# A convolution's last loop step and three seams in a fused decoder trunk: splits, operators, squares and a norm moved

## The chip, the cores and the metric

The kernel runs on one core of a Trainium2 chip. The metric is the device time of one execution in microseconds (us). The engines are named as the profile does: PE (TensorE, matrix products; PEld its weight loads), DVE (VectorE), ACT (ScalarE), POOL (GpSimd) and SP (SyncE), whose queue issues the DMA transfers here. Each engine executes its own instructions in the order in which they were written, and waits on semaphores for others.

## The reference: two macaron layers

The reference takes x of 512 tokens x 1024 channels in float32 through two layers. Each is a half-step SwiGLU feed-forward, a token mixer, and another half-step feed-forward. The mixer of layer 0 is S5, a diagonal complex state-space layer; the one of layer 1 is a Conformer convolution. Every sublayer is normed before and after:

```python
def rmsnorm(x, g):
    y = xf * lax.rsqrt(jnp.mean(xf * xf, axis=-1, keepdims=True) + EPS)
    return (y * g).astype(x.dtype)

def conv_mixer(h, w_in, b_in, dw, dw_b, ln_g, ln_b, w_out, b_out):
    a, g = jnp.split(h @ w_in + b_in, 2, axis=-1)
    z = a * jax.nn.sigmoid(g)
    z = depthwise_conv(z, dw, width 31, causal) + dw_b
    z = jax.nn.silu(layernorm(z, ln_g, ln_b))
    return z @ w_out + b_out

for i in range(2):
    x = x + 0.5 * rmsnorm(swiglu(rmsnorm(x, pre[i, 0]), ...), post[i, 0])
    x = x + rmsnorm(mixer(rmsnorm(x, pre[i, 1])), post[i, 1])
    x = x + 0.5 * rmsnorm(swiglu(rmsnorm(x, pre[i, 2]), ...), post[i, 2])
```

(The call of the depthwise convolution is shortened.) So six sublayers follow each other: ffn0, s5, ffn2, ffn3, conv, ffn5. The numbers are those of the norms' weights.

## The kernel before

**Layout.** x stays on the chip as eight tiles of 128 channels x 512 tokens. Channels lie on partitions, so a product is `weights^T x activations` into one of 8 PSUM banks (tiles named ps, 128x512). A pool of 39 pages (pg) holds weights and activations alike, 3 raw buffers (raw) take weights as they are loaded.

**Three matmuls per product.** Weights come in units of 128x1024 floats (512 KB), loaded by SP (L90, `raw<-`w). ACT rounds a unit to a high page (L101, a cast), DVE subtracts it from the raw one to get a low page (L105). `want(n)` does this for all units up to n, in the order of the program, and asks for the loads of the three units behind each; a raw buffer is free for the next load once the subtraction has read it. Activations are split likewise: ACT makes the high part (L180), DVE the low one (L193). `mm3` (L117 to L119) then issues high x high, high x low and low x high.

**A sublayer's entry.** The first products run on x times the norm's weights, before the norm's factor is known; it is one factor y per token, multiplied in when the products leave PSUM. For it the squares of x are summed over the eight tiles on ACT (L184) and DVE (L189), `entry_norm` sums them over partitions with a matmul by ones (`stat`, L124), and three DVE steps (L132 to L134) make y.

**The seams.** `proj` is a sublayer's last product and its passage to the next. It makes 8 output tiles of 512 tokens, the last `nl` of them in two halves of 256 tokens, A and B (`nl` is 1 in the feed-forwards, 2 in S5 and the convolution). While PE does the B halves, the post-norm's stat of half A runs, and then a loop over `s` takes each half tile through scaling (`scaled`, L358), the addition to x (`added`, L362), the split into high and low part (L180, L193), and the next sublayer's first products (`entry_step`). A product's square is summed by `evac` (L273 on ACT, L278 on DVE), its values copied from PSUM by `copy` (L284, or L286 with a bias). The argument `defer` tells where the squares for the next entry norm are made: if true, behind the loop, with full width, after one more split of weights; if false, in the loop, by halves. It is true where the next sublayer is a feed-forward, which leaves it false from ffn0 to s5 and from ffn3 to conv. The work that ffn, s5 and conv hand on is in the result: pages xn, banks ps, the squares' sum acc2.

**The convolution.** Its input product gives 8 pairs of tiles (pa, pb), one per channel tile. The first two pairs are made in the seam; the loop over i = 2..7 makes the others, and runs `gate(i-1)` behind the products of step i: DVE multiplies both by y (L1148, L1150), ACT makes a sigmoid (L1149), DVE multiplies (L1153 or L1164). Tiles 0, 1 and 7 are convolved on DVE, tap by tap (`taps_dve`, L1177 to L1183, the last 5 taps of tile 7 on PE by diagonal matrices, L1194). Tiles 2 to 6 go through DRAM to be laid out anew (`z_d`, written at L1154, read at L1159), are multiplied on PE with banded matrices (`banded`, L1286, 36 matmuls of 128x128 each; the matrices are loaded by `operators`, L1277, in five transfers), leave PSUM by ACT (`unstack`, L1297) and go through DRAM again (`c_d`, L1305 and L1306, by `fetch`). `step(n)` runs n taps, `finish` and `accumulate` the sums for the layer norm. A gate's z_d and z reads, `fetch` and `operators` all issue on SP, which waits in order.

In the last step, i = 7, the order before is: products of pair 7 with the banded product of tile 4 between its two parts, `operators(5)`, `operators(6)`, `want(u0 + 19)`, `fetch`, `gate(6)`, `finish`, taps, `accumulate`, `unstack` of tile 4. `want(u0 + 19)` splits the first four units of the output weights (units 16 to 19) and asks for the loads of 19 to 22. After the loop come the banded products of tiles 5 and 6, `gate(7)`, the remaining taps and sums, and the layer norm's end: L1389 adds the last tile's parts, L1253 sums them over partitions on PE, and `lead` feeds the output projection through ACT's SiLU and copy (L1427, L1429) and DVE's low part (L1440).

Of the kernel before, what the change touches and what calls it, by code (L numbers as in the profile page):

```python
# [41 lines left out]
def trunk(ctx: ExitStack, tc: tile.TileContext, h, plan):  # L42
# [209 lines left out]

    def proj(u0, nk, rhs, post, nl, pre, xn, bias=None, lead=None, carried=None, defer=True, early=False):

# [69 lines left out]
        for m in last:  # L324
# [4 lines left out]
            copy(m, ps, A)  # L329
        psb = {}  # L330
        for i, (m, k) in enumerate((m, k) for m in last for k in range(nk)):
            if i == 5:
                sa = stat(acc[:, A])
                steps = rsqrt_steps(sa, y[:, A], carried is None)
                if pre is not None:
                    lo_engine[0] = None
                    want(un + 3)
                    lo_engine[0] = DVE
                for f in steps:
                    f()  # L340
            if k == 0:
                psb[m] = psum()[:, :n]
            product(m, k, psb[m], B)
            if k == nk - 1 and m != NK - 1:
                evac(m, psb[m], B)
                copy(m, psb[m], B)
        pb = psb[NK - 1]
# [23 lines left out]
        for s in range(len(todo) + 2):  # L371
# [9 lines left out]
            if 1 <= s <= len(todo):  # L381
                added(*todo[s - 1])
            if s == 4:
                sq = square(NK - 1, pb, B)
# [17 lines left out]
        if defer:  # L402
            want(un + 4)
            for k in range(NK):
# [53 lines left out]

    def ffn(e, post, pre, defer=True, early=False):
        u0, xn = e["u"], e["xn"]  # L460
# [667 lines left out]
    def conv(e, post, pre):  # L1128
# [197 lines left out]
        for i in range(2, NK):  # L1326
            want(u0 + 2 * i + 1)
            pa, pb = psum(), psum()
            for j, ps in enumerate((pa, pb)):
                for k in range(NK):  # L1330
                    mm3(ps, u0 + 2 * i + j, k, xn[k][:, 0, :], xn[k][:, 1, :], k == 0, k == NK - 1)
                    if i == 2 and j == 0 and k == 4:
                        entry_norm(e)
                if j == 0 and i - 3 in banks:
                    done = banded(i - 3)
            if i - 2 in banks and i > 4:
                operators(i - 2)
            if i == NK - 1:
                operators(i - 1)
            want(u0 + 2 * i + (3 if i < NK - 1 else 5))  # L1340
            if i == 2:
# [13 lines left out]
            if done:  # L1355
                unstack(*done)
                done = None
        done = [banded(i) for i in banks[-2:]]
        fetch()
# [119 lines left out]
    for i, (kind, idx) in enumerate(subs):  # L1479
        pre = subs[i + 1][1] * 8 if i + 1 < len(subs) else None  # L1480
        post = 48 + idx * 8
        if kind == "ffn":
            after = subs[i + 1][0] if i + 1 < len(subs) else "ffn"
            e = ffn(e, post, pre, after == "ffn", after == "s5")
        elif kind == "s5":
# [104 lines left out]
```

## Time and profile before

| what | value |
|---|---|
| median of 3 runs | 1881.44 us (1881.33 to 1881.71) |
| the profiled execution | 1881.37 us |
| its span in the trace | 1879.6 us |
| TensorE busy in it | 1861.2 us |
| mean granted TensorE clock | 0.998 of full |
| ffn3, from 964.0 to 1328.95 | 364.95 us, PE busy 364.31 |
| conv, from 1328.95 to 1528.73 | 199.78 us, PE busy 193.56, DVE 169.16 |

The execution is some 1.8 us longer than its span, what lies before the first and behind the last instruction. Times in the trace count from the start of the span. A sublayer is taken here from the first full-width product behind a seam to the same point of the next one. A row of a timeline has the start, the length, the engine, the line in the kernel, the operation, the tile that it writes and those that it reads (pool names without their number), how many instructions stand together, and in brackets how long the engine was idle before it and what released it. Successive instructions of an engine overlap a little, so the time of one is read from one start to the next. "SPq" is SP's queue: its rows are the issuing of transfers, not the transfers themselves.

### The profile page before, as it was taken

What the parts mean: (1) busy time and instruction counts of PE and PEld (TensorE: products, weight loads), DVE (VectorE), ACT (ScalarE), POOL (GpSimd) and SP (SyncE); (2) the same over time, 40 slices, a digit from 0 to 9 for tenths busy, and PEclk for the clock granted to TensorE, in tenths of its full rate; (3) what the DMA queues carried; (4) which work ended last, traced back from release to release, by engine and by line L of the source; (5) the groups of instructions that cost most, each with busy time, mean ns of one, the idle gap of its engine ahead of it and who ended that gap; (6) DMA issues with size and microseconds to landing.
All of it is one profiled execution on the core that took longest, in us unless ns stands there. A gap on an engine that the chain in (4) does not pass through costs nothing.

```text
span 1879.6 us, 24042 instructions
## 1 busy us (share of the span) xinstructions
PE 1861.2 (99%) x9498; PEld 1588.4 (85%) x9498; DVE 1079.2 (57%) x1907; ACT 639.1 (34%) x931; POOL 30.5 (2%) x56
## 2 busy tenths in 40 slices
PE   9999999999999999999999999999999999999998
PEld 7888888888989888888898888888887988888887
DVE  6888556789658543332485433325988775433324
ACT  5232545242245432221344222213413543222211
POOL 0000000003100000000000000000000000000000
PEclk9999999999999999999999999999999999999999
DMA  5344448849422423222223332222473224332321
GB/s 164 113 138 155 146 124 256 279 148 353 152 90 79 135 90 110 92 78 90 102 78 124 102 100 82 95 92 79 163 282 107 79 74 129 97 105 79 95 96 46
DMA packets 101809, 234.87 MB, mean 125 GB/s; under 512 B 26176, under 2 KB 45120, under 8 KB 101696
## 3 DMA queue, kind: packets, MB, share of 16 engines
q1 hardware_dynamic: 101552, 233.31, 38.0%
q8 instruction: 74, 1.21, 0.3%
q14 instruction: 39, 0.32, 0.1%
q10 hardware_dynamic: 144, 0.02, 0.0%
HBM read 209.58 MB, written 23.72 MB: 124 GB/s over the span
## 4 chain that ended last, share of the span: by engine, by line
PE 83%; DVE 12%; ACT 2%; issue 2%; DMA 1%; SPq 0%; DVEq 0%; ACTq 0%
PE ps L118 26%; PE ps L119 26%; PE ps L117 26%; DVE pg L105 1%; DVE pg L697 1%; PE ps L1286 1%; PE ps L976 1%; DVE pg L1183 1%; PE ps L792 1%; DVE pg L527 1%; DVE tmp L467 1%; PE ps L124 1%; ACT tmp L466 1%; DVE pg L699 1%; ACT pg L469 1%
## 5 line engine op out<-in xcount | busy, mean ns | idle before, releaser
L117 PE MATMUL ps<-pg,pg 128*128 128x512 f32 (+1 forms) x2808 | 1035.6, 369 | 4.5 <-ACT pg L1429 3.9
L118 PE MATMUL ps<-pg,pg 128*128 128x512 f32 (+1 forms) x2808 | 1030.8, 367 | 4.5 <-DVE pg L193 3.7
L119 PE MATMUL ps<-pg,pg 128*128 128x512 f32 (+1 forms) x2808 | 1028.5, 366 | 0.2 <-DVE pg L105 0.2
L118 PEld LDWEIGHTS ps<-pg,pg 128*128 128x128 f32 x2808 | 530.7, 189 | 94.7 <-DVE pg L193 7.5
L117 PEld LDWEIGHTS ps<-pg,pg 128*128 128x128 f32 x2808 | 530.8, 189 | 91.5 <-ACT pg L1429 4.3
L119 PEld LDWEIGHTS ps<-pg,pg 128*128 128x128 f32 x2808 | 530.6, 189 | 85.8 <-DVE pg L105 0.9
L105 DVE TENSOR_TENSOR pg<-raw,pg 128x1024 fp32r<-128x1024 f32 x305 | 361.2, 1222 | 106.2 <-ACT pg L101 68.0
L101 ACT CAST pg<-raw 128x1024 fp32r<-128x1024 f32 x310 | 311.4, 1047 | 107.3 <-PE ps L118 28.4
L467 DVE TENSOR_TENSOR tmp<-ps,tmp 128x512 f32<-128x512 f32 x88 | 60.9, 692 | 247.6 <-PE ps L119 218.4
L278 DVE TENSOR_TENSOR acc<-acc,tmp 128x512 f32<-128x512 f32 (+1 forms) x53 | 32.6, 615 | 250.1 <-ACT tmp L273 250.0
L466 ACT ACTIVATE tmp<-tmp 128x512 f32<-128x512 f32 x88 | 55.6, 632 | 287.0 <-DVE tmp L465 287.0
L469 ACT CAST pg<-tmp 128x512 fp32r<-128x512 f32 x88 | 54.6, 621 | 251.2 <-DVE tmp L467 249.4
L273 ACT ACTIVATE tmp<-ps 128x512 f32<-128x512 f32 (+1 forms) x45 | 24.2, 539 | 285.3 <-PE ps L119 284.9
L470 DVE TENSOR_TENSOR pg<-tmp,pg 128x512 fp32r<-128x512 f32 x88 | 61.0, 693 | 61.7 <-ACT pg L469 61.7
L465 DVE TENSOR_TENSOR tmp<-ps,y 128x512 f32<-128x512 f32 x88 | 60.6, 689 | 27.4 <-PE ps L119 27.4
L180 ACT ACTIVATE pg<-x,gsc 128x256 fp32r<-128x256 f32 x80 | 40.7, 509 | 68.1 <-DVE x L362 68.1
L1183 DVE SCALAR_TENSOR_TENSOR pg<-pg,vec,pg 128x512 f32<-128x512 f32 x82 | 55.4, 755 | 0.0
L193 DVE SCALAR_TENSOR_TENSOR pg<-x,gsc,pg 128x256 fp32r<-128x256 f32 (+1 forms) x88 | 44.8, 509 | 2.6 <-ACT pg L180 1.4
L1286 PEld LDWEIGHTS ps<-pg,pg 128*128 128x128 f32 x360 | 40.8, 192 | 0.3
L1286 PE MATMUL ps<-pg,pg 128*128 128x128 f32 x360 | 40.8, 275 | 0.0
L362 DVE SCALAR_TENSOR_TENSOR x<-tmp,gsc,x 128x256 f32<-128x256 f32 x80 | 38.8, 485 | 0.0
L976 PE MATMUL ps<-pg,pg 128*128 128x128 f32 x256 | 35.0, 277 | 1.2 <-DVE pg L962 0.9
(165 smaller groups left out, 828.6 us busy)
## 6 DMA issues: line engine op xcount, KB each, us to landing
raw<-w SPq DMA_DIRECT2D x262, 512.0 KB, 4.0
pg<-tab_d SPq DMA_DIRECT2D x24, 512.0 KB, 5.9
pg<-toep SPq DMA_DIRECT2D x20, 512.0 KB, 6.1
tab_d<-pg SPq DMA_DIRECT2D x16, 512.0 KB, 4.4
raw<-cv_w_in SPq DMA_DIRECT2D x16, 512.0 KB, 4.2
pg<-s5b SPq DMA_DIRECT2D x8, 512.0 KB, 6.5
pg<-f_d SPq DMA_DIRECT2D x32, 128.0 KB, 5.9
raw<-s_w_in SPq DMA_DIRECT2D x8, 512.0 KB, 3.8
```

The lines of the kernel that those rows point to most:

```text
L101: ACT.copy(hv, r)
L105: lo_engine[0].tensor_tensor(lv, r, hv.bitcast(F32), op=ALU.subtract)
L117: PE.matmul(out, lhsT=hi[:, s, :], rhs=xh, start=start, stop=False)
L118: PE.matmul(out, lhsT=hi[:, s, :], rhs=xl, start=False, stop=False)
L119: PE.matmul(out, lhsT=lo[:, s, :], rhs=xh, start=False, stop=stop)
L465: DVE.tensor_tensor(a, pa, e["y"], op=ALU.mult)
L466: ACT.activation(a, a, AF.Silu)
L467: DVE.tensor_tensor(a, pb, a, op=ALU.mult)
L469: ACT.copy(t[:, 0, :], a)
L470: DVE.tensor_tensor(t[:, 1, :], a, t[:, 0, :].bitcast(F32), op=ALU.subtract)
L1183: DVE.scalar_tensor_tensor(a, v, dw(i, w), a, op0=M, op1=A)
L1286: PE.matmul(ps[:, q * P : q * P + P], lhsT=op[ND * q + d], rhs=z[:, q, 8 - d : 8 - d + P], start=d == 0, stop=d == ND - 1,)
```

## The change

There are four parts.

1. `defer` becomes a number: 4 where it was true, 0 from ffn0 to s5, and 5 from ffn3 to conv, where it was false. There the squares leave the loop and come behind it at full width, after two splits.
2. The convolution's `entry_norm` is called at j = 1, k = 6 of step i = 2 rather than at j = 0, k = 4, which is ten products, 30 matmuls, later.
3. In seams with `nl` = 2 the first half's stat is called behind three products of the B halves rather than five, and the sum and copy of the first of the two B halves come in the loop at s = 2, not ahead of it. Its square is still made when the product ends.
4. In the convolution's last step `operators(6)` and `want(u0 + 19)` move behind `gate(6)`, `finish`, the taps, `accumulate` and `unstack`.

```diff
--- before.py
+++ after.py
@@ -250,7 +250,7 @@
 
         rsqrt(stat(e["acc2"][:, HALVES[1]]), e["y"][:, HALVES[1]])
 
-    def proj(u0, nk, rhs, post, nl, pre, xn, bias=None, lead=None, carried=None, defer=True, early=False):
+    def proj(u0, nk, rhs, post, nl, pre, xn, bias=None, lead=None, carried=None, defer=4, early=False):
 
         acc = stat_tile() if carried is None else carried
         acc2 = stat_tile()
@@ -327,9 +327,9 @@
                 product(m, k, ps, A)
             evac(m, ps, A)
             copy(m, ps, A)
-        psb = {}
+        psb, behind = {}, []
         for i, (m, k) in enumerate((m, k) for m in last for k in range(nk)):
-            if i == 5:
+            if i == (5 if nl == 1 else 3):
                 sa = stat(acc[:, A])
                 steps = rsqrt_steps(sa, y[:, A], carried is None)
                 if pre is not None:
@@ -342,8 +342,7 @@
                 psb[m] = psum()[:, :n]
             product(m, k, psb[m], B)
             if k == nk - 1 and m != NK - 1:
-                evac(m, psb[m], B)
-                copy(m, psb[m], B)
+                behind.append((m, square(m, psb[m], B)))
         pb = psb[NK - 1]
         if pre is None:
             assert bias is None and carried is not None
@@ -380,6 +379,10 @@
                 more.pop(0)()
             if 1 <= s <= len(todo):
                 added(*todo[s - 1])
+            if s == 2 and behind:
+                m, sq = behind.pop()
+                plus(sq, B)
+                copy(m, psb[m], B)
             if s == 4:
                 sq = square(NK - 1, pb, B)
                 plus(sq, B)
@@ -400,7 +403,7 @@
             if s == 5:
                 side = rsqrt_steps(sb, y[:, B], carried is None)
         if defer:
-            want(un + 4)
+            want(un + defer)
             for k in range(NK):
                 x_plus(x_square(k, FULL, acc2), FULL, acc2)
         return {"xn": xn, "ps": ps4, "acc2": acc2, "u": un, "y": ye}
@@ -456,7 +459,7 @@
         for k in range(LAST_PE, NK):
             added(B, k)
 
-    def ffn(e, post, pre, defer=True, early=False):
+    def ffn(e, post, pre, defer=4, early=False):
         u0, xn = e["u"], e["xn"]
         g = []
 
@@ -1329,15 +1332,14 @@
             for j, ps in enumerate((pa, pb)):
                 for k in range(NK):
                     mm3(ps, u0 + 2 * i + j, k, xn[k][:, 0, :], xn[k][:, 1, :], k == 0, k == NK - 1)
-                    if i == 2 and j == 0 and k == 4:
+                    if i == 2 and j == 1 and k == 6:
                         entry_norm(e)
                 if j == 0 and i - 3 in banks:
                     done = banded(i - 3)
             if i - 2 in banks and i > 4:
                 operators(i - 2)
-            if i == NK - 1:
-                operators(i - 1)
-            want(u0 + 2 * i + (3 if i < NK - 1 else 5))
+            if i < NK - 1:
+                want(u0 + 2 * i + 3)
             if i == 2:
                 ACT.preload_act_table(AF.Sigmoid)
                 for n in range(2):
@@ -1355,6 +1357,9 @@
             if done:
                 unstack(*done)
                 done = None
+            if i == NK - 1:
+                operators(i - 1)
+                want(u0 + 2 * i + 5)
         done = [banded(i) for i in banks[-2:]]
         fetch()
         gate(*pend)
@@ -1481,7 +1486,7 @@
         post = 48 + idx * 8
         if kind == "ffn":
             after = subs[i + 1][0] if i + 1 < len(subs) else "ffn"
-            e = ffn(e, post, pre, after == "ffn", after == "s5")
+            e = ffn(e, post, pre, {"ffn": 4, "conv": 5, "s5": 0}[after], after == "s5")
         elif kind == "s5":
             e = s5(e, post, pre)
         else:
```

Lines of the changed kernel behind the seam are three further on: L1148 is L1151 there, L1154 L1157, L1277 L1280, L1183 L1186; in the seam `scaled` is L357 and `added` L361.

DVE in the convolution's last step, before: the sum of a tile's two tap halves (L1186), four weight splits, then gate 6 (the two products L1148 and L1150, the gated product L1153 and the clearing of the margin L1156).

```order
L1186 TENSOR_TENSOR pg_10482<-pg_10599 128x512
L105 TENSOR_TENSOR pg_11177<-raw_10878,pg_11176 128x1024
L105 TENSOR_TENSOR pg_11183<-raw_11017,pg_11182 128x1024
L105 TENSOR_TENSOR pg_11189<-raw_11023,pg_11188 128x1024
L105 TENSOR_TENSOR pg_11195<-raw_11180,pg_11194 128x1024
L1148 TENSOR_TENSOR tmp_11206<-ps_10917,y_10541 128x512
L1150 TENSOR_TENSOR tmp_11205<-ps_10916,y_10541 128x512
L1153 SCALAR_TENSOR_TENSOR tmp_11205<-tmp_11205,vec,tmp_11206 128x512
L1156 MEMSET pg_11212 128x4x8
```

The same place in the changed order, from gate 6 (its second product, L1153) to the start of gate 7 (L1151 on the banks of pair 7); between them lie the sums for the layer norm (L1228 to L1249) and the splits.

```order
L1153 TENSOR_TENSOR tmp_11149<-ps_10894,y_10549 128x512
L1156 SCALAR_TENSOR_TENSOR tmp_11149<-tmp_11149,vec,tmp_11150 128x512
L1159 MEMSET pg_11156 128x4x8
L1230 TENSOR_TENSOR pg_10472<-pg_10472,acc_10476 128x512
L1228 SCALAR_TENSOR_TENSOR pg_10473<-pg_10473,vec,acc_10476 128x512
L1248 TENSOR_TENSOR pg_10477<-pg_10472,pg_10473 128x512
L1249 TENSOR_TENSOR pg_10477<-pg_10477,tmp_11166 128x512
L105 TENSOR_TENSOR pg_11185<-raw_10856,pg_11184 128x1024
L105 TENSOR_TENSOR pg_11191<-raw_10995,pg_11190 128x1024
L105 TENSOR_TENSOR pg_11197<-raw_11001,pg_11196 128x1024
L105 TENSOR_TENSOR pg_11203<-raw_11188,pg_11202 128x1024
L1151 TENSOR_TENSOR tmp_11288<-ps_11048,y_10549 128x512
```

The four splits stood ahead of gate 6 and now stand ahead of gate 7.

SP's queue at the same place, before: the last operator of the second set, four loads of output weights, then the banded tile's way through DRAM (c_d) and that of gate 6's z.

```order
L1277 DMA pg_11174<-toep 128x512
L90 DMA raw_11180<-cv_w_out 128x1024
L90 DMA raw_11186<-cv_w_out 128x1024
L90 DMA raw_11192<-cv_w_out 128x1024
L90 DMA raw_11198<-cv_w_out 128x1024
L1305 DMA c_d<-pg_11067 32x4x128 x4
L1306 DMA pg_10483<-c_d 128x512
L1154 DMA z_d<-tmp_11205 128x512
L1159 DMA pg_11212<-z_d 32x4x128 x4
```

And in the changed order, up to the first load of output weights:

```order
L1308 DMA c_d<-pg_11045 32x4x128 x4
L1309 DMA pg_10473<-c_d 128x512
L1157 DMA z_d<-tmp_11149 128x512
L1162 DMA pg_11156<-z_d 32x4x128 x4
L1354 DMA pg_11168<-diag 128x640
L1280 DMA pg_11174<-toep 128x1024
L1280 DMA pg_11176<-toep 128x1024
L1280 DMA pg_11178<-toep 128x1024
L1280 DMA pg_11180<-toep 128x1024
L1280 DMA pg_11182<-toep 128x512
L90 DMA raw_11188<-cv_w_out 128x1024
```

The second set of operators and the loads have moved behind c_d, z_d, the z reads and the diagonals. raw_11188 is the page that the last of the four splits reads (pg_11203 on DVE above).

DVE in the seam from conv to ffn5, before: the post-norm's factor of half A (L132 to L134), the sum and copy of the first B half (L278, L286), then the loop (L358, L362, L193).

```order
L132 SCALAR_TENSOR_TENSOR tmp_11920<-tmp_11919 128x256
L133 SCALAR_TENSOR_TENSOR tmp_11920<-ps_11917,tmp_11920 128x256
L134 SCALAR_TENSOR_TENSOR y_11842<-tmp_11920,tmp_11919 128x256
L278 TENSOR_TENSOR acc_11443<-acc_11443,tmp_11939 128x256
L286 TENSOR_SCALAR pg_11448<-ps_11901,vec 128x256
L358 TENSOR_TENSOR tmp_11972<-pg_11445,y_11842 128x256
L358 TENSOR_TENSOR tmp_11974<-pg_11445,y_11842 128x256
L362 SCALAR_TENSOR_TENSOR x<-tmp_11972,gsc,x 128x256
```

In the changed order:

```order
L134 SCALAR_TENSOR_TENSOR y_11820<-tmp_11892,tmp_11891 128x256
L357 TENSOR_TENSOR tmp_11948<-pg_11423,y_11820 128x256
L357 TENSOR_TENSOR tmp_11950<-pg_11423,y_11820 128x256
L361 SCALAR_TENSOR_TENSOR x<-tmp_11948,gsc,x 128x256
L357 TENSOR_TENSOR tmp_11954<-pg_11424,y_11820 128x256
L361 SCALAR_TENSOR_TENSOR x<-tmp_11950,gsc,x 128x256
L278 TENSOR_TENSOR acc_11421<-acc_11421,tmp_11917 128x256
L286 TENSOR_SCALAR pg_11426<-ps_11879,vec 128x256
L193 SCALAR_TENSOR_TENSOR pg_11413<-x,gsc,pg_11413 128x256
```

The sum and copy now stand behind the second addition to x.

## The prediction

> **What bounds the kernel now.** The page's first lines come first: one engine is busy almost throughout.
>
> ```profile
> span 1879.6 us, 24042 instructions
> PE 1861.2 (99%) x9498; PEld 1588.4 (85%) x9498; DVE 1079.2 (57%) x1907; ACT 639.1 (34%) x931; POOL 30.5 (2%) x56
> ```
>
> TensorE (PE) works 1861.2 of 1879.6 us, so a change can gain little more than the 18 us in which PE waits, and loses whatever it adds to them. The profiled execution took 1881.37 us, 1.8 above its span; the median is 1881.44, so sums made in the trace are added to 1881.4. The waits of PE, grouped by releaser (total us, times, mean), put them in two places that the change touches:
>
> ```profile
> PE ps L117 <- ACT pg L1429: 3.9, 1, 3.9
> PE ps L118 <- DVE pg L193: 3.7, 11, 0.6
> ```
>
> L1429 is at the end of the convolution, L193 in the seams between sublayers. The windows view gives two seams of one kind, from the first half-row matmul to the last, each with 8 products left and right (columns: length, then busy time and count of PE, weight loads, VectorE (DVE), ScalarE (ACT), GpSimd, then granted clock, DMA share, GB/s):
>
> ```profile
> 924.34:964.05 39.71, 39.71 (x329) 39.60 (x328) 32.37 (x70) 20.92 (x36) 0.00 (x0) 1.00 0.21 68
> 1287.30:1328.95 41.65, 41.02 (x330) 39.95 (x329) 34.67 (x80) 22.77 (x45) 0.00 (x0) 1.00 0.16 52
> ```
>
> The same 329 or 330 matmuls take 39.71 us from ffn2 to ffn3, where PE is never idle, and 41.65 us from ffn3 to the convolution, where DVE is busy 34.67 us with 10 instructions more (the halves of the squares' sums). A half-row matmul is 39.71/329 = 0.121 us. Full-row ones come from a steady stretch:
>
> ```profile
> 700.00:800.00 100.00, 100.00 (x443) 82.85 (x442) 41.11 (x47) 29.66 (x38) 0.00 (x0) 1.00 0.30 95
> ```
>
> 100/443 = 0.226 us each. In the convolution PE looks full, but three stretches tell which engine sets the end:
>
> ```profile
> 1336.40:1401.55 65.15, 65.15 (x360) 56.38 (x360) 63.87 (x96) 15.40 (x19) 0.00 (x0) 1.00 0.69 239
> 1401.55:1420.41 18.86, 18.86 (x122) 16.98 (x121) 9.35 (x13) 4.82 (x7) 0.00 (x0) 1.00 0.79 301
> 1420.41:1447.15 26.74, 26.74 (x185) 23.58 (x184) 26.43 (x40) 6.33 (x9) 0.00 (x0) 1.00 0.38 102
> ```
>
> From gate 0 (1336.40) to 1401.55 DVE is busy 63.87 of 65.15 us; from gate 7 (1420.41) to L1389 (1447.15), 26.43 of 26.74. Only in between does it idle, half of the time. What follows hangs on DVE (the rows of PE around it):
>
> ```profile
> 1406.72 8.20 PE L1286 MATMUL ps<-pg,pg 128*128 128x128 f32 x72
> ...
> 1447.83 0.70 PE L1253 MATMUL ps<-pg,ones 128*128 128x256 f32 x2 [0.17 <-DVE pg L1389]
> ...
> 1453.76 0.58 PE L117 MATMUL ps<-pg,pg 128*128 128x256 f32 x1 [3.86 <-ACT pg L1429]
> ```
>
> L1253 adds the last sums after L1389, and the projection's first matmul (L117) waits 3.86 us for ACT at 1453.76. Thus whatever delays gate 7 delays the projection by as much, since 26.4 of the 26.7 us behind it are DVE's own work in its own order. Gate 7's surroundings on DVE:
>
> ```profile
> 1406.75 1.22 DVE L105 TENSOR_TENSOR pg<-raw,pg 128x1024 fp32r<-128x1024 f32 x1 [2.83 <-issue]
> 1413.76 1.22 DVE L105 TENSOR_TENSOR pg<-raw,pg 128x1024 fp32r<-128x1024 f32 x1 [5.78 <-ACT pg L101]
> 1414.90 0.68 DVE L1148 TENSOR_TENSOR tmp<-ps,y 128x512 f32<-128x512 f32 x1
> ...
> 1416.38 0.75 DVE L1153 SCALAR_TENSOR_TENSOR tmp<-tmp,vec,tmp 128x512 f32<-128x512 f32 x1 [0.19 <-ACT tmp L1149]
> ...
> 1420.41 0.69 DVE L1148 TENSOR_TENSOR tmp<-ps,y 128x512 f32<-128x512 f32 x1 [0.62 <-PE ps L119]
> 1447.15 1.15 DVE L1389 TENSOR_TENSOR pg<-pg 128x256 f32<-128x256 f32 x2
> ```
>
> Before gate 6 (1414.90) DVE waited 2.83 + 5.78 us for two splits (L105, 1414.90 - 1413.76 = 1.14 us from one to the next), and gate 7 still had to wait 0.62 us for its own products. That idle time cost nothing: PE, not DVE, released gate 7.
>
> **The change part by part.**
>
> *Seam from ffn3 to the convolution.* The 16 half squares and 14 half sums leave it and come afterwards as 8 and 7 of full width. It becomes the seam of the other row: 39.71 - 41.65 = **-1.94 us**. It has the same count of matmuls and that one has no wait, so I take this without a margin. The squares' sums come behind two splits, before the moved stat needs them.
>
> *Seams with two last products (s5 to ffn2, conv to ffn5).* The first half's stat goes two products ahead: 6 x 0.121 = 0.72 us. Two DVE instructions also leave the place ahead of the scaling:
>
> ```profile
> 573.09 0.42 DVE L278 TENSOR_TENSOR acc<-acc,tmp 128x256 f32<-128x256 f32 x1
> 573.42 0.42 DVE L284 COPY pg<-ps 128x256 f32<-128x256 f32 x1
> ```
>
> They cost 573.09 to about 573.76 (0.33 us from one to the next, 0.67 for both), but come back two steps later in the same chain on DVE, so they gain nothing by themselves. DVE's chain starts up to 0.72 us sooner. From nothing to -1.3 each (0.72, with most of the 0.67 on top, if their new place lies in an idle moment); I take -0.6 and -0.5, nearest to the stat's own move. **-1.1 us**, between 0 and -2.6.
>
> *The convolution's entry norm.* Its stat moves behind 30 more matmuls, 30 x 0.226 = 6.8 us. The loop itself begins 1.94 earlier, so y and gate 0 come 4.84 us later: 1341.24. The next rows of DVE:
>
> ```profile
> 1336.40 0.69 DVE L1148 TENSOR_TENSOR tmp<-ps,y 128x512 f32<-128x512 f32 x1
> ...
> 1342.88 2.36 DVE L105 TENSOR_TENSOR pg<-raw,pg 128x1024 fp32r<-128x1024 f32 x2
> ```
>
> The two splits at 1342.88 stand behind gates 0 and 1, so they come at 1347.7 and end 1.2 us apart. PE reaches their unit after two steps of 48 matmuls, 1328.95 - 1.94 + 96 x 0.226 = 1348.7 us, plus about 1 us of stat, and uses the lo page third: about a microsecond to spare. PE isn't stopped, and DVE, busy at 98%, carries the 4.84 us on: gate 6, which no longer has splits ahead of it, starts at 1401.55 + 4.84 = 1406.4, and ends (its L1153 ended 2.2 us after its start) at 1408.6.
>
> *The last step's operators and splits behind gate, taps and sums.* Gate 6 loses 8.6 us of waiting and nobody needs it sooner. What counts is the fourth split: it stands on DVE directly ahead of gate 7, and its raw page is loaded behind all that now goes first on SP. SP's queue before:
>
> ```profile
> 1384.82 3.12 SPq L1305 DMA_DIRECT2D c_d<-pg  x4
> ...
> 1390.94 0.38 SPq L1154 DMA_DIRECT2D z_d<-tmp  x1
> 1394.35 1.75 SPq L1159 DMA_DIRECT2D pg<-z_d  x4
> 1396.14 5.54 SPq L1277 DMA_DIRECT2D pg<-toep  x10
> 1402.81 12.53 SPq L90 DMA_DIRECT2D raw<-cv_w_out  x4
> ```
>
> At 1384.82 the four c_d writes begin, and z_d follows 1390.94 - 1384.82 = 6.12 us later, since the c_d read between waits for the writes' landing. Then the z reads come 3.41 after z_d and take 1.75. In the changed order: z of gate 5 is 4.84 later, its reads end at 1396.14 + 4.84 = 1401.0, five operator loads (half of 5.54) end at 1403.8, and c_d starts there. 6.1 later would be 1409.9; with the operators (4.5 pages of 512 KB) still in flight ahead I take z_d of gate 6 at 1410.5. Reads at 1413.9, the diagonals at 1415.7, five operators from 1416.2 to 1418.9, and only then the raw page. Its buffer is no obstacle: ACT's copy of the banded product (L1297) waits for PE, 1406.72 + 8.20 - 1.94 = 1413.0; then come 0.57 of copy, 1.05 of cast and 1.2 of the first split, 1415.9. How long does the load take? Two rows bound it. In a quiet place a chain through one raw page reads:
>
> ```profile
> 524.59 1.06 ACT pg L101
> ...
> 525.72 1.24 DVE pg L105
> ...
> 526.98 3.49 DMA raw<-s_w_out
> ...
> 530.49 1.06 ACT pg L101
> ...
> 531.58 1.24 DVE pg L105
> ```
>
> 3.49 us alone, then 1.06 for the cast and 1.14 for the split. But behind the ten operators ACT waited for it until 1412.68:
>
> ```profile
> 1412.68 1.05 ACT L101 CAST pg<-raw 128x1024 fp32r<-128x1024 f32 x1 [10.28 <-DMA raw<-cv_w_out]
> ...
> 1418.97 0.57 ACT L1297 COPY pg<-ps 128x512 f32<-128x512 f32 x1
> ```
>
> Issued at 1402.81, that took 9.8 us. The transfer rate over the stretch from 1360 to 1425 (40 slices) shows why:
>
> ```profile
> GB/s 60 152 282 413 401 390 352 349 32 67 125 277 416 421 318 305 222 257 27 57 266 37 147 214 411 421 413 421 418 412 413 415 303 23 55 339 90 125 208 38
> ```
>
> While loads are queued they get up to 421 GB/s and no more: 512 KB in 1.25 us, and 3.49 - 1.25 = 2.24 us of the lone load are not transfer. If they are served in order, the diagonals (128x640, 0.8 us), 4.5 pages of operators (5.6 us) and the raw page (1.25 us) follow each other from 1415.7 + 2.24 = 1417.9 and end at 1425.6; at 1425.0 with z_d at 1409.9, and at 1427.1 if SP or the queue loses 1.5 us more. I take 1426.0, about 7.1 us from issue, between 3.49 and 9.8. With 1.06 + 1.14 gate 7 starts at **1428.2 instead of 1420.41: +7.8 us**. This replaces the 1.94 of the first seam and the 4.84 (both lie ahead of gate 7 and end in it); only the -1.1 is added, 0.6 of it earlier in all these times alike.
>
> The Trainium skill ("DMA: Bandwidth & Descriptors", Anatomy of one DMA) puts a transfer at a fixed part of about 2 us plus bytes over some 436 GB/s, by my estimate 3.2 us for 512 KB. The trace's 3.49 agrees nearly, and its 9.8 shows that the queue counts for more. By that figure the sum would be the first rival's, 0.3 us lower.
>
> *PE's clock in the wait.* Gate 7 being late leaves PE with little between its last banded product and L1253. After the 3.86 us wait before the projection the granted clock is halved:
>
> ```profile
> 1456.00:1458.00 2.00, 2.00 (x11) 2.00 (x10) 2.00 (x7) 1.67 (x4) 0.00 (x0) 0.50 0.00 0
> ```
>
> If the late sums already meet it, the two L1253 matmuls (0.70 us) take twice as long: between 0 and +0.7. I take **+0.4**: the pauses are longer in all than the one in the row, but are cut by single matmuls. The Trainium skill ("TensorE: Matmul & The Clock Gate", What's actually happening) says that the clock falls to half once an idle window of about 3.4 us has passed; the row agrees. With shorter pauses than that its rule would give 0, and the sum would be 0.4 lower.
>
> The sum: 7.8 - 1.1 + 0.4 = +7.1, **1888.5 us**. The ends: landing -1.0 or +1.1, seams -1.5 or +1.1, clock -0.4 or +0.3, give +4.2 to +9.6, 1885.6 to 1891.0.
>
> **The rivals.**
>
> *The load isn't queued.* If the raw page doesn't wait on SP or behind the operators, it is issued when its buffer is free, 1415.9, and lands 3.49 later; with 2.2 gate 7 is at 1421.6, +1.2. With -1.1 that is +0.1: **1881.5, no change**. For: 3.49 in the quiet place, and sixteen DMA engines. Against: the order on SP, and 9.8 us in the very same step. Chance 0.14.
>
> *DVE no longer sets the end* (the other side: not slower). The waits for splits that leave gate 6 (8.6 us) would then be worth something, and PE alone would count: -1.94 - 1.1, 1878.4, with the best seams 1876.9, **faster or unchanged**. This decides if DVE's stretch behind gate 7 can shrink by the 7.8 us, for instance if its sums have been done earlier. Against: the stretch is 99% busy and in both orders holds the same work. Chance 0.05, of it 0.03 under the bound for faster.
>
> *Slower still.* SP also waits for free pages before the second set of operators, or PE loses the microsecond of margin and its clock. Another 3 us gives **1891.5**. The operators' pages are freed by banded products that end at 1413.0, before SP asks for them. Chance 0.05.
>
> **How the numbers follow.** Main case 0.76, the rivals 0.14, 0.05, 0.05. A measurement of this kernel can tell about 0.2% from no change: 3.8 us. The main case (+4.2 to +9.6) and the third rival are slower: 0.81. The first rival and the rest of the second are no change: 0.16. Faster: 0.03. The range goes from the first rival's end, 1881.4, to the main case's upper end, 1891.0; the main case alone is 1885.6 to 1891.0.
>
> **What would show it right or wrong.** In the changed trace the fourth L105 of the last step should stand directly ahead of gate 7, released by a cast that waited for its DMA, at about 1427, with DVE idle there for some 8 us, not ahead of gate 6. The raw page's issue should come after ten z, diagonal and operator issues at 1418.9 and land 6 to 8 us later. The projection's first matmul should be near 1461.5 (1453.76 + 7.8), less 0.6. The seam into the convolution should measure 39.7 us, the two others about half a microsecond less than before. The prediction is wrong if gate 7 is released by PE at about 1419, if the load lands within 4 us of its issue, or if DVE has idle time between gate 7 and L1389 to give the delay back.

## The result, and the profile after

The changed kernel takes 1892.69 us (median of 4 runs, 1892.09 to 1894.36) against 1881.56 before: a ratio of 1.0061, 95% interval 1.0048 to 1.0074, or 11.1 us more. The forecast was 1888.5 with a range up to 1891.0: slower, as forecast, but by more. The profiled execution took 1893.18 us with a span of 1891.4, 11.8 longer than before.

The waits of PE (total, times, longest) show where PE stands idle now. The projection waits as before; new is the wait of the sums (L1256, before L1253) for DVE:

```profile
PE ps L1256 <- DVE pg L1228: 7.6, 2, 6.7
PE ps L117 <- ACT pg L1434: 3.9, 1, 3.9
```

DVE in the last step, from gate 6 on:

```profile
1405.90 0.69 DVE L1151 TENSOR_TENSOR tmp<-ps,y 128x512 f32<-128x512 f32 x1
...
1414.02 3.50 DVE L105 TENSOR_TENSOR pg<-raw,pg 128x1024 fp32r<-128x1024 f32 x3 [3.18 <-ACT pg L101]
1431.08 1.22 DVE L105 TENSOR_TENSOR pg<-raw,pg 128x1024 fp32r<-128x1024 f32 x1 [13.57 <-ACT pg L101]
1432.23 0.68 DVE L1151 TENSOR_TENSOR tmp<-ps,y 128x512 f32<-128x512 f32 x1
...
1458.84 1.14 DVE L1394 TENSOR_TENSOR pg<-pg 128x256 f32<-128x256 f32 x2
```

The prediction named this picture: no idle time ahead of gate 6, the fourth split directly ahead of gate 7 and released by a cast, DVE idle before it. The sizes differ: it said some 8 us of idle time and a split at about 1427, and the trace has 13.57 us and 1431.08, with gate 7 at 1432.23 (before 1420.41). The work from there to L1394 takes 26.61 us (26.74 before). ACT's cast ahead of that split:

```profile
1430.01 1.04 ACT L101 CAST pg<-raw 128x1024 fp32r<-128x1024 f32 x1 [14.12 <-DMA raw<-cv_w_out]
```

The cast waited 14.12 us for its load. SP's queue tells why it was so late:

```profile
1389.19 1.90 SPq L1308 DMA_DIRECT2D c_d<-pg  x4
...
1396.92 0.38 SPq L1157 DMA_DIRECT2D z_d<-tmp  x1
...
1402.09 3.31 SPq L1280 DMA_DIRECT2D pg<-toep  x5
1405.49 2.39 SPq L1308 DMA_DIRECT2D c_d<-pg  x4
1412.56 0.34 SPq L1309 DMA_DIRECT2D pg<-c_d  x1
1412.99 0.38 SPq L1157 DMA_DIRECT2D z_d<-tmp  x1
1416.38 1.75 SPq L1162 DMA_DIRECT2D pg<-z_d  x4
1418.17 0.43 SPq L1354 DMA_DIRECT2D pg<-diag  x1
1418.64 2.62 SPq L1280 DMA_DIRECT2D pg<-toep  x5
1421.36 11.31 SPq L90 DMA_DIRECT2D raw<-cv_w_out  x4
```

First c_d writes and z of gate 5, then the operators of tile 5, c_d writes, c_d read, z of gate 6, z reads, diagonals, operators of tile 6, and only then the load (1421.36). The read (1412.56) waits for the writes to land, the z reads (1416.38) for z.

The three seams after, and the two that the prediction did not quote before (columns as in the prediction):

```profile
563.04:600.52 37.48, 36.34 (x293) 35.56 (x292) 33.17 (x73) 21.67 (x38) 0.00 (x0) 1.00 0.22 73
1286.73:1326.44 39.71, 39.71 (x329) 39.60 (x328) 32.23 (x69) 20.94 (x36) 0.00 (x0) 1.00 0.22 74
1502.68:1540.54 37.86, 36.52 (x294) 35.56 (x293) 33.79 (x74) 22.12 (x38) 0.00 (x0) 1.00 0.23 82
```

```profile
563.13:601.10 37.97, 36.50 (x294) 35.57 (x293) 33.10 (x73) 21.57 (x38) 0.00 (x0) 1.00 0.21 71
1490.51:1528.73 38.22, 36.54 (x293) 35.55 (x292) 33.75 (x74) 21.99 (x38) 0.00 (x0) 1.00 0.23 77
```

The seam into the convolution went from 41.65 to 39.71, the others by 0.49 and 0.36.

The 11.8 us of the span: gate 7 later by 1432.23 - 1420.41 = 11.82; from there to the projection's first matmul 33.20 after 33.35, -0.15; the projection to the last seam's start 37.25 after 36.75, +0.50; the last seam -0.36; behind it nothing. (The gain of the two earlier seams lies ahead of gate 7 and is part of its 11.82.)

### The profile page after: what moved, and what is told of

Its sections match the earlier page's. It is cut to its first block, busy times and chain, and to the rows that moved or that the text cites. A ratio compares the mean times of both kernels' runs of the same rounds, so it can differ in the third digit from the quotient of the medians.

```text
span 1891.4 us, 24032 instructions
## 1 busy us (share of the span) xinstructions
PE 1864.0 (99%) x9498; PEld 1589.6 (84%) x9498; DVE 1078.7 (57%) x1900; ACT 638.4 (34%) x923; POOL 30.6 (2%) x56
## 4 chain that ended last, share of the span: by engine, by line
PE 83%; DVE 11%; ACT 2%; DMA 2%; issue 2%; SPq 0%; DVEq 0%; ACTq 0%
PE ps L118 26%; PE ps L119 26%; PE ps L117 26%; DVE pg L105 2%; DVE pg L700 1%; PE ps L979 1%; PE ps L1289 1%; DVE pg L1186 1%; PE ps L795 1%; DVE pg L530 1%; DVE tmp L470 1%; PE ps L124 1%; ACT tmp L469 1%; DVE pg L702 1%; DVE tmp L468 0%
## 5 line engine op out<-in xcount | busy, mean ns | idle before, releaser
L278 DVE TENSOR_TENSOR acc<-acc,tmp 128x512 f32<-128x512 f32 (+1 forms) x53 | 32.6, 614 | 249.1 <-ACT tmp L273 249.0
L1186 DVE SCALAR_TENSOR_TENSOR pg<-pg,vec,pg 128x512 f32<-128x512 f32 x82 | 55.1, 739 | 0.0
L193 DVE SCALAR_TENSOR_TENSOR pg<-x,gsc,pg 128x256 fp32r<-128x256 f32 (+1 forms) x88 | 44.2, 503 | 1.9 <-ACT pg L180 1.5
L361 DVE SCALAR_TENSOR_TENSOR x<-tmp,gsc,x 128x256 f32<-128x256 f32 x80 | 38.2, 478 | 0.0
```

Of the source, the lines that this page charges most:

```text
L1186: DVE.scalar_tensor_tensor(a, v, dw(i, w), a, op0=M, op1=A)
```

## The experiments

The theory of the prediction (theory 1): the fourth split's load stands last in SP's queue, and gate 7 waits for it. Theory 2: the late entry norm is the cost. Theory 3: the four splits' own 4.6 us on DVE ahead of gate 7. All runs are beside runs of the kernel before on the same chip. The rows without "part" or "before" in their name are edits of the changed kernel, the rows with a part's number have these parts alone. The last column is the convolution's own stage in the profiled execution, from its first full-width matmul to the projection's first. It is of one execution each, which can lie off the median: that of half of part 2 took 1888.67 us and that of the early load 1883.98, each the longest of its ten; that of the four buffers took 1887.63, the shortest of its five.

| kernel | median, us | before, us | ratio, 95% | stage, us |
|---|---|---|---|---|
| before | | | | 124.81 |
| the change (1 2 3 4) | 1892.69 | 1881.56 | 1.0048-1.0074 | 138.99 |
| load asked for early, four buffers | 1882.11 | 1881.78 | 0.9993-1.0012 | 131.89 |
| four buffers | 1889.07 | 1881.78 | 1.0026-1.0055 | 135.28 |
| load ahead of operators | 1884.89 | 1881.78 | 1.0007-1.0026 | 130.93 |
| parts 1 2 3 | 1890.28 | 1881.78 | 1.0031-1.0061 | 136.38 |
| parts 1 3 4 | 1883.67 | 1881.62 | 1.0002-1.0020 | 129.19 |
| parts 1 3 | 1878.94 | 1881.62 | 0.9977-0.9995 | 124.71 |
| part 4 | 1886.08 | 1881.62 | 1.0015-1.0035 | 130.26 |
| part 2 | 1892.47 | 1881.62 | 1.0045-1.0072 | 134.81 |
| part 2, load early, four buffers | 1887.22 | 1881.85 | 1.0014-1.0039 | 130.96 |
| part 2, four buffers | 1885.55 | 1881.85 | 1.0010-1.0029 | 128.82 |
| half of part 2 | 1884.95 | 1881.85 | 1.0013-1.0032 | 131.76 |
| part 3 | 1880.87 | 1881.85 | 0.9983-1.0002 | 124.91 |
| the change, operators on ACT's queue | 1895.39 | 1881.68 | 1.0059-1.0086 | 141.86 |
| part 2, operators on ACT's queue | 1894.49 | 1881.68 | 1.0048-1.0079 | 138.69 |
| before, four buffers | 1880.99 | 1881.68 | 0.9985-1.0003 | 124.72 |
| parts 1 3, operators on ACT's queue | 1880.18 | 1881.68 | 0.9989-1.0007 | 125.54 |

**The load asked for early**, on the changed kernel (memory holds a fourth raw buffer only with one page less):

```diff
-    pages = ctx.enter_context(tc.tile_pool(name="pages", bufs=39))
-    rawp = ctx.enter_context(tc.tile_pool(name="rawp", bufs=3))
+    pages = ctx.enter_context(tc.tile_pool(name="pages", bufs=38))
+    rawp = ctx.enter_context(tc.tile_pool(name="rawp", bufs=4))
...
             if i < NK - 1:
                 want(u0 + 2 * i + 3)
+            else:
+                w_dma(u0 + 2 * i + 5)
```

> The changed kernel with four raw buffers in place of three (and 38 pages in place of 39), and the load of the fourth output unit asked for ahead of gate 6, where the four splits stood before; the splits and operators stay behind the gate. Theory 1 (the fourth split's load, last in SP's queue, holds gate 7): the load has landed long before, the four splits run on in one go from 1414.0 (4 x 1.15), gate 7 starts at about 1418.6 instead of 1432.2, and the time falls to 1879.5 to 1881.0. Theory 2 (the late entry norm alone makes DVE late): no change, 1892.7. Theory 3 (the four splits' own time on DVE, 4.6 us ahead of gate 7): the splits still stand there, so it stays above 1886.

Measured 1882.11. DVE:

```profile
1412.40 4.63 DVE L105 TENSOR_TENSOR pg<-raw,pg 128x1024 fp32r<-128x1024 f32 x4 [2.91 <-ACT pg L101]
1416.94 0.68 DVE L1151 TENSOR_TENSOR tmp<-ps,y 128x512 f32<-128x512 f32 x1
...
1436.68 0.75 DVE L1228 SCALAR_TENSOR_TENSOR pg<-pg,vec,acc 128x512 f32<-128x512 f32 x1 [6.43 <-DMA pg<-c_d]
```

The four splits run on in 4.54 us and gate 7 starts at 1416.94, 15.3 earlier than in the changed kernel; so the load had held it, and the splits' own time (theory 3) does not cost what was measured. But the time is a microsecond or more above the expectation. In the profiled execution a new wait of 6.43 us for the banded tiles' way back from DRAM stands behind gate 7: the c_d writes land at 1433.29 to 1433.87, right behind three loads that SP issued before them (the last landed at 1433.07). SP's queue had a second customer.

**Its control**, the four buffers without the early call:

> The control of the early load: the changed kernel with four raw buffers and 38 pages, the load where the change puts it. Theory 1: SP's order is the changed kernel's, so the load still lands at about 1430 and the time stays at 1892.7, give or take 1. Theory 2: 1892.7 as well. If the missing raw buffer or a page were what holds gate 7, the time would fall to 1880 or move by several us.

1889.07: 3.6 less than expected, with the fourth split still waiting 9.78 us. Of the 10.6 us between the change and the early load, buffers alone can claim up to 3.6.

**One split and its load ahead of the second operators:**

```diff
+                want(u0 + 2 * i + 2)
                 operators(i - 1)
                 want(u0 + 2 * i + 5)
```

> The changed kernel with only the first of the four splits ahead of the second set of operators, so that the load that it asks for is issued before them. Theory 1: issued at about 1418.6, it waits only for the diagonals (0.8 us) and lands at 1422.5 to 1423.5; gate 7 starts at 1425, 7 us earlier, and the time is 1885, give or take 1. Theory 2: 1892.7. Theory 3: 1892.7, since DVE has the same splits ahead of gate 7.

1884.89. DVE:

```profile
1413.54 3.50 DVE L105 TENSOR_TENSOR pg<-raw,pg 128x1024 fp32r<-128x1024 f32 x3 [3.17 <-DMA pg<-c_d]
1422.50 1.23 DVE L105 TENSOR_TENSOR pg<-raw,pg 128x1024 fp32r<-128x1024 f32 x1 [5.47 <-ACT pg L101]
1423.64 0.68 DVE L1151 TENSOR_TENSOR tmp<-ps,y 128x512 f32<-128x512 f32 x1
```

Same bytes, same buffers, another order in the queue: gate 7 at 1423.64, 8.6 earlier. Order decides here. Theories 2 and 3 fall as full accounts of the change; what the norm costs by itself is measured below.

**The parts alone and in pairs.** Without part 4 (its two lines put back):

> The changed kernel without part 4: operators and splits of the last step ahead of gate 6 again, the entry norm still late. Theory 1 in its strict form: the chain on SP begins with gate 5's z, which the late norm puts 6 us later than before (1396.9 against 1390.9); the fourth load then lands at about 1418.5, gate 6 starts at 1420.8 and gate 7 at 1426, and the time is 1887, give or take 1. Theory 2: the norm is all, 1892. If part 4 alone were the cost and the late norm had 8 us of idle time to hide in, as DVE's idle time in the profile before suggests: 1879.5.

1890.28, above even the strict form:

```profile
1417.99 1.23 DVE L105 TENSOR_TENSOR pg<-raw,pg 128x1024 fp32r<-128x1024 f32 x1 [8.27 <-ACT pg L101]
1419.13 0.68 DVE L1151 TENSOR_TENSOR tmp<-ps,y 128x512 f32<-128x512 f32 x1
...
1452.37 0.75 DVE L1228 SCALAR_TENSOR_TENSOR pg<-pg,vec,acc 128x512 f32<-128x512 f32 x1 [4.92 <-DMA pg<-c_d]
```

```profile
PE ps L1289 <- DMA pg<-z_d: 7.6, 1, 7.6
```

The fourth load now holds gate 6 (1419.13), as the strict form said, but the chain goes on from there: gate 6's z reaches PE 7.6 us late for the banded product of tile 6, and its result holds DVE for 4.92 us. Part 4 adds only about 2.6 us (11.1 - 8.5) to this.

> The changed kernel with the entry norm where it was (parts 1, 3 and 4 remain). Theory 1 (the fourth split's load, last in SP's queue): the queue's chain starts with gate 5's z, now at about 1388.7; the second operators are issued by 1412.3, the load at 1415.2 when its buffer is free; it lands at about 1420.5 behind the operators, gate 7 starts at 1422.7, 2.3 later than before, less 0.4 for the last seam: 1883.7, between 1882.5 and 1885. Theory 2 (the late norm is the cost, splits behind the gate cost nothing): 1879. Theory 3 (the four splits' own DVE time ahead of gate 7): 1886 or more.

1883.67, with gate 7 at 1422.84 as expected:

```profile
1421.69 1.23 DVE L105 TENSOR_TENSOR pg<-raw,pg 128x1024 fp32r<-128x1024 f32 x1 [3.72 <-ACT pg L101]
1422.84 0.68 DVE L1151 TENSOR_TENSOR tmp<-ps,y 128x512 f32<-128x512 f32 x1
```

> Parts 1 and 3 alone: the seams changed, the norm and the last step as before. All theories: the three seams give 1.94 + 0.49 + 0.37 = 2.8 us, if the norm's stat finds its sums made when PE comes to it (DVE ends them at 1329.7 and PE comes at 1329.9 in the changed kernel's trace): 1878.9, between 1878.3 and 1880. If the late squares hold the stat, PE waits some tenths more.

1878.94, faster than both kernels. PE releases gate 7 again:

```profile
1411.28 1.22 DVE L105 TENSOR_TENSOR pg<-raw,pg 128x1024 fp32r<-128x1024 f32 x1 [5.89 <-ACT pg L101]
...
1417.84 0.69 DVE L1151 TENSOR_TENSOR tmp<-ps,y 128x512 f32<-128x512 f32 x1 [0.52 <-PE ps L119]
```

> The kernel before with part 4 alone. Theory 1: gate 5's z goes out at 1390.9 as before, the operators of the second set by 1414, the load lands at about 1422 and gate 7 starts at 1424.2, 3.8 later than before, with some tenths for the clock: 1885.8, give or take 1. Theory 2: 1881.7, since the norm is where it was. Theory 3: 1886.

1886.08: part 4 costs 4.5 us by itself. Theories 1 and 3 had both given this time, so the time does not tell them apart. The trace does: it is not the splits' own work but the fourth split's wait for its cast that stands ahead of gate 7 (1425.18).

```profile
1424.04 1.23 DVE L105 TENSOR_TENSOR pg<-raw,pg 128x1024 fp32r<-128x1024 f32 x1 [4.78 <-ACT pg L101]
```

> The kernel before with the later entry norm alone. Gate 0 comes 6.8 us later, and so does gate 5's z on SP. If the fourth load, behind ten operators, is 6 us later as in the run without part 4, gate 6 starts at about 1421 and gate 7 at 1426, and the banded tiles' way through DRAM, which follows gate 6's z on SP, comes later too: 1891 to 1894 (theory 2, and the strict form of theory 1). If the 8.6 us in which DVE waits ahead of gate 6 can hide the norm, as the prediction took it: 1881.7 to 1882.5.

1892.47: the norm by itself costs 10.9 us, more than the 6.8 us by which it moves. DVE, and PE's wait:

```profile
1420.29 1.23 DVE L105 TENSOR_TENSOR pg<-raw,pg 128x1024 fp32r<-128x1024 f32 x1 [8.57 <-ACT pg L101]
1421.43 0.68 DVE L1148 TENSOR_TENSOR tmp<-ps,y 128x512 f32<-128x512 f32 x1
...
1426.24 0.68 DVE L1148 TENSOR_TENSOR tmp<-ps,y 128x512 f32<-128x512 f32 x1
...
1452.93 0.75 DVE L1225 SCALAR_TENSOR_TENSOR pg<-pg,vec,acc 128x512 f32<-128x512 f32 x1 [3.39 <-DMA pg<-c_d]
```

```profile
PE ps L1286 <- DMA pg<-z_d: 6.5, 1, 6.5
```

Gate 7 is only 5.8 us later (1426.24). Most of the rest comes from the banded product of tile 6, which waits 6.5 us for z, and from its result, for which DVE waits 3.39 us. The idle time ahead of gate 6 (8.57 us) has not become shorter although DVE came later: the load it waits for came later as well. The trace shows on what this load hung. Before, SP issued it at 1402.81, when an earlier transfer had landed that shares its semaphore (the third of the ten operators, 1402.53) and the first of the four splits on DVE had freed its buffer (1402.78). With the late norm the two came at 1410.48 and 1409.45, and the load went out at 1410.55. The split is late with DVE (6.67 us), the operator with gate 5's z, which stands ahead of it on SP and goes out at 1398.08 instead of 1390.94. So that idle time was no room for the norm.

> The kernel before with the entry norm later by half: 15 matmuls, 3.4 us, in place of 30. Theory 1: before, gate 7 had 0.6 us to spare and the z of tile 6 about as little; all beyond goes into the time one to one or somewhat more, as in the whole step (6.8 us cost 10.9): 1885, between 1884 and 1887. If DVE's 8.6 us of idle time hid it, as the prediction took it: 1881.6 to 1882.

1884.95. Half the move costs 3.1 us: there is no room of 8 us.

**The norm alone, with the load early and four buffers** (the same edits, the call ahead of the operators of tile 5):

> The kernel before with the later entry norm, four raw buffers (38 pages), and the load of the fourth output unit asked for ahead of both sets of operators. Theory 1 (SP's queue carries the norm's lateness: fourth load, then gate 6's z, then the banded tiles): the four splits run on from 1408.2 and gate 6 starts at 1412.9 instead of 1421.4; what is left is the c_d and z of gate 6 behind ten operators and the loads, and a banded product that still waits some us for its z: 1884 to 1887, some 6 us below the norm alone. Theory 2 (DVE's own lateness): no change, 1892.5.

1887.22, at the upper end. DVE and SP:

```profile
1407.02 4.61 DVE L105 TENSOR_TENSOR pg<-raw,pg 128x1024 fp32r<-128x1024 f32 x4
1411.56 0.67 DVE L1148 TENSOR_TENSOR tmp<-ps,y 128x512 f32<-128x512 f32 x1
...
1419.11 0.69 DVE L1148 TENSOR_TENSOR tmp<-ps,y 128x512 f32<-128x512 f32 x1 [2.67 <-PE ps L119]
...
1447.85 0.75 DVE L1225 SCALAR_TENSOR_TENSOR pg<-pg,vec,acc 128x512 f32<-128x512 f32 x1 [3.17 <-DMA pg<-c_d]
```

```profile
1401.83 7.30 SPq L1277 DMA_DIRECT2D pg<-toep  x10
1410.03 2.19 SPq L90 DMA_DIRECT2D raw<-cv_w_out  x3
1413.05 3.99 SPq L1305 DMA_DIRECT2D c_d<-pg  x4
1422.88 0.34 SPq L1306 DMA_DIRECT2D pg<-c_d  x1
1423.32 0.38 SPq L1154 DMA_DIRECT2D z_d<-tmp  x1
```

Gate 6 is free at 1411.56 and gate 7 is released by PE (1419.11). Yet z of gate 6 goes out at 1423.32, ten us after its gate, behind the c_d writes, which land behind ten operators and three loads. The fourth load is one customer of the queue; z and c_d are another.

> Its control: the later entry norm with four raw buffers and 38 pages, the load where the kernel before has it, behind the operators. Theory 1: the fourth load still lands behind ten operators, at about 1419; 1889 to 1892.5, since four buffers let earlier loads out of the way of the writes to DRAM, as they did in the other control (3.6 us). If a buffer were all: as the run with the early load.

1885.55, below the expectation and not above the run with the early load. So theory 1 was wrong about the fourth load here: it landed at 1415.42 and not at 1419.

```profile
1416.61 1.23 DVE L105 TENSOR_TENSOR pg<-raw,pg 128x1024 fp32r<-128x1024 f32 x1 [6.72 <-ACT pg L101]
...
1422.57 0.68 DVE L1148 TENSOR_TENSOR tmp<-ps,y 128x512 f32<-128x512 f32 x1
```

A fourth buffer lets each load go out one split earlier and takes it out of the way of later transfers: z of gate 5 goes out at 1394.22 (with part 2 alone 1398.08), the fourth load at 1405.76 (1410.55), the c_d writes ahead of gate 6's z at 1411.11 (1422.22). Asking for one load ahead of the operators adds nothing to that here. In the two profiled executions (1884.74 and, with part 2 alone, 1892.43) the 7.7 us divide in two: gate 7 is 3.67 us earlier (1422.57 and 1426.24), and behind it DVE's waits for c_d, 0.69 and 3.39 us with part 2 alone, are gone.

> The kernel before with four raw buffers and 38 pages, the control of the controls. With the norm late, four buffers saved 7 us; if they save by shortening SP's queue ahead of a late step, nothing is late here and nothing is saved: 1881.3 to 1882.3. If four buffers help by themselves: 1878 or less.

1880.99 (0.9985 to 1.0003): without a late norm the buffers give 0.7 us, which is not told from nothing.

**The operators on another queue** (`nc.scalar.dma_start` for `toep`):

> The changed kernel with the operators' loads issued from ACT's queue in place of SP's; nothing else moves. Theory 1 (one queue, in order): the c_d writes and the fourth load no longer stand behind operators; gate 6's z goes out when it is ready (1408), the load is issued when its buffer is free (1416) and lands by 1420, gate 7 starts at 1421 to 1423, ten us earlier: 1881.5 to 1885. Rival (bandwidth: the same bytes come at the same 421 GB/s by whichever queue): 1890 or more.

> The kernel before with the later entry norm alone, and the operators' loads on ACT's queue. Theory 1: the norm's cost of 10.9 us goes through SP's queue, so most of it goes: 1882 to 1886. Rival (bandwidth): 1890 or more. If DVE itself were late by the norm's 6.8 us: 1888.

1895.39 and 1894.49, each 2 to 3 us slower than with the operators on SP's queue. Both miss theory 1's range and lie where the rival had put them. ACT in the first:

```profile
1417.67 9.08 ACTq L1280 DMA_DIRECT2D pg<-toep  x4
1426.85 2.94 ACT L101 CAST pg<-raw 128x1024 fp32r<-128x1024 f32 x3 [11.81 <-DMA pg<-z_d]
```

ACT itself is held for 9.08 us issuing four operators, and its casts come after. In the trace each of these issues follows the landing of an earlier transfer of SP (a c_d read at 1417.57, z at 1419.50, two z reads at 1425.86 and 1426.14). So the edit put a new wait on ACT; it does not tell order from bandwidth, which only the load put first does.

> Parts 1 and 3 alone, with the operators' loads on ACT's queue. With the norm early PE released gate 7 (0.52 us of waiting for it in the trace), so the queue has nothing to give: 1878.9, between 1878.2 and 1879.6. If the issuing holds ACT up: slower by some us.

1880.18 (1878.08 to 1886.03), above the expected range and no gain over 1878.94.

**Part 3 alone:**

> The kernel before with part 3 alone (the earlier stat and the later sum and copy in the two seams with two last products). The prediction's estimate is -1.1 us; the lengths of these seams in the changed kernel's trace say -0.49 and -0.37: 1880.7, between 1880.2 and 1881.2.

1880.87, -1.0 (ratio 0.9983 to 1.0002): in line with the 0.85 of the two seams, and not told from nothing by time alone.

## Why the prediction was wrong, point by point

- **The seam into the convolution**, -1.94: 39.71 us measured, right. **The two others**, -1.1 forecast: 0.49 + 0.36 = 0.85 measured; right but for 0.25.
- **y and gate 0** at 1341.24 less 0.6: measured 1340.69. **Gate 6** at 1406.4 less 0.6: 1405.90. PE did not stop at the split behind gates 0 and 1. All right.
- **The load's landing**, forecast at 1426.0 less 0.6, measured at 1429.98: this is the step that failed, and it made the number wrong by 4.6 us; the sum was 4.7 short of the profiled execution (7.1 against 11.8). The wait and its place were right, the price of SP's queue was too low in four terms, each against the forecast less 0.6. z of gate 5 went out 1.7 late (1396.92), since the c_d writes ahead of it, issued from 1389.19, landed behind two loads (1394.75) and were down only at 1396.35. Five operators took 3.31 us to issue, not 2.77. z of gate 6 followed the first c_d write by 7.5 us (1405.49 to 1412.99), not 6.7. And from issue to landing it was 8.6 us, not 7.1. I had reckoned the queue ahead of the load, but not the queue ahead of the steps that lead to it. Why the last term was 1.5 us too small stays open (see the gaps in the last section). The fixed part of about 2 us that the prediction gives from the Trainium skill ("DMA: Bandwidth & Descriptors", Anatomy of one DMA) is fitted there to transfers that GpSimd issues. These loads are SP's; the sum used the 3.49 us of the trace in its place.
- **What sets the end**: DVE behind gate 7, 26.6 us, right. **The clock**: the granted clock was halved, as expected, after a long pause of PE (0.50 from 1446.21 to 1447.50):

```profile
1434.94 4.56 PE L1197 MATMUL ps<-pg,pg 128*128 128x512 f32 x10 [0.99 <-DVE pg L1167]
1446.21 1.22 PE L1256 MATMUL ps<-pg,ones 128*128 128x256 f32 x2 [6.71 <-DVE pg L1228]
```

Two matmuls of L1256 take 1.22 us there. But on the path nothing was lost: L1394 to the projection's first matmul is 6.59 us (6.61 before), because the clock is back by then (the pair at 1459.50 takes 0.70 us, as in the kernel before). The +0.4 was wrong there. The +0.50 of the projection goes with the clock too: the half-row matmuls at its start took 26.35 us at a mean granted clock of 0.88, before 25.84 at 0.90. Over all the traces this stretch took 25.37 (clock 0.93) to 26.80 us (0.87). So the +0.4 stood in the wrong place, and that it is near the 0.50 is chance. The Trainium skill ("TensorE: Matmul & The Clock Gate", What's actually happening) has the clock fall after an idle window of about 3.4 us; the 6.71 us here agree.
- **What the cost was put down to.** The prediction's +7.8 is one chain for parts 1, 2 and 4 together. The norm's 4.84 us stands in it as the lateness of gate 5's z on SP; no part has a price of its own. Of gate 6's 8.6 us of waiting it says only that "nobody needs it sooner". The expectations of the experiments went further and read it as if DVE's idle time could hide the norm. That reading falls: parts 1 to 3 cost 8.5 us where they would have gained about 3, and part 2 alone costs 10.9. Of the 8.6 us, 5.78 were a wait for a load, whose issue hangs on the same late gates in two ways, through SP's queue and through the buffer that DVE frees: a late norm moves this wait along and does not eat into it. The other 2.83, ahead of the third split, ended with a matmul of PE (1406.67). With part 2 alone that wait is gone, but the wait for the load has grown to 8.57.
- **The rivals**: a load that isn't queued is refuted by 8.6 us from issue to landing. The second (DVE's stretch shrinks) by 26.61 us. "Slower still" (1891.5) came nearest in time, and one of its causes shows: of the five operators of 3.31 us, the third took 1.36 us to issue, where the first two took 0.43 each, and a matmul of PE released it, so about 0.9 us may be a wait for a page. Most of the excess was queueing.

## What to carry to other kernels

Idle time ahead of an instruction is room only if what ends it doesn't depend on the thing that you delay: follow the releaser back through its queue to its first link. A queue that waits in order makes neighbours of transfers that have nothing to do with each other; price a transfer by what stands ahead of it and by each wait for a landing, not by its own length. And try the parts one by one: here two gains (parts 1 and 3, -2.7 us) were buried under a norm that cost 10.9 and a move that cost 4.5 alone but 2.6 on top.

## What the runs showed of the hardware

Within a run of loads that land 1.2 to 1.3 us apart, one landed late: in the changed kernel two operators landed at 1422.85 and 1425.68, 2.83 apart. The DMA queues of 1421 to 1423 (packets, MB, share of 16 engines):

```profile
q1 hardware_dynamic: 155, 0.57, 102.1%
q8 instruction: 1, 0.02, 3.6%
```

One packet of instructions took 3.6% of 16 engines for 2 us, 1.15 us of one of them. In the kernel before, a gap of 2.58 us (1408.17 to 1410.75) has such a packet just ahead of it (1407.82). But there are gaps without a packet of this queue: 1.99 us in the changed kernel (1406.38 to 1408.37) and 2.70 with the early load (1407.32 to 1410.02). That the packet makes the gap was not tested; if it does, it is 1.3 to 1.6 us of the error.

The trace shows the transfers of this program signal eight semaphores in turn, over both queues, and an issue can wait until the transfer eight places before it has landed. The four c_d writes at 1413.05 above were issued at 1413.05, 1414.29, 1415.53 and 1416.74, each about 0.02 us after an operator landed (1413.03, 1414.28, 1415.51, 1416.72). So they took 3.99 us; in the changed kernel those at 1389.19 took 1.90. I had not reckoned with that either.
